# The weights of two wide input products, from the fifth pair on, fetched through ScalarE's DMA queue

## The chip, the cores and the metric

The kernel runs on one core of one Trainium2 chip. The time is the device time of one execution in microseconds; of three runs the median is shown. Lower is better. The core's engines are TensorE (PE, its weight loads PEld), VectorE (DVE), ScalarE (ACT), GpSimd (POOL) and SyncE (SP), which issues all DMAs of this kernel before the change. Each engine takes its instructions strictly in its own order.

## The reference, cut to what matters

Two transformer blocks follow each other on 1024 tokens of width 1024, all in float32: gated linear attention with a pooling branch and a gated feed-forward, then an mLSTM with latent attention and a squared-ReLU MLP. The change touches the first product of each feed-forward part:

```python
gate, up = jnp.split(h2 @ w_ffn_in[l], 2, axis=-1)      # 1024 x 1024 by 1024 x 5632
x = x + (jax.nn.silu(gate) * up) @ w_ffn_out[l]
...
y = jnp.square(jax.nn.relu(m @ w_up[l])) @ w_down[l]    # m @ w_up: 1024 x 1024 by 1024 x 4096
x = x + rmsnorm_2(y, norm_post_mlp[l])
```

## The kernel before, in words

Every float32 factor is split into a high part (rounded to the matmul's format) and the low rest, and a product is three matmuls: high by high, high by low, low by high (`mm3`, lines 117 to 119). The split is a cast on ACT (line 94) and a subtraction on DVE (line 95).

`wide_in` (line 754) does the two wide input products. It is called at line 925 for `w_ffn_in` ("feed-forward" below, 22 pairs of panels) and at line 1687 for `w_up` ("up" below, 16 pairs). A pair is a block of 256 columns of the weight, 1 MB, loaded by one DMA into the tile `raw` (`load`, line 769). The product of the 2 x 2 blocks is done in seven block products of 12 matmuls each, by a scheme that adds and subtracts blocks first. They run in four units: P1 and P2, P5 and P6, P3 and P7, P4 (`UNITS`). Their left operands come from the weight (`operands`): unit 0 from `raw` itself, units 1 and 2 from the sums `s` that POOL makes of blocks of `raw` (lines 808 to 812), unit 3 from `raw`. Each is split into a tile `wo`. The other operands are the blocks of the activations (tiles `b` for P1, P2, P3, tiles `T` for P5, P6, P7, P4), which is how a row of PE shows where P2 ends: the matmul after it reads a `T`.

`product` takes each result out of PSUM, for which there are four banks in turn: P1 and P5 by a copy on ACT into `t` (line 827), P2 by DVE with P1 added (line 832), P6 by DVE (836) with a sum on POOL behind it (838), P3 by DVE with that sum added (841), P7 by DVE (845) and POOL (847), P4 by DVE (851). So DVE's line 841 needs POOL's line 838. Four finished blocks of a pair go through `consume`: in feed-forward a tanh on ACT (line 917) or a product with the gate (line 922), in up a ReLU on ACT and a square on DVE (lines 1683 and 1684). Then `spill_hidden` adds and subtracts them (lines 895 to 905, DVE) and spills seven tiles of 256 KB to DRAM (line 886, `f_scr<-g`) for the product that comes next; in feed-forward every second pair does so.

The program order is that of the loop at line 858: operands run two units ahead of their products, the units 0 of the first four pairs (`PRE`) run first, and the load of the next pair is written ahead of unit 2 (line 865). A scheduler then orders each engine's instructions by a timeline of its own. The tiles `raw` and `wo` come from two pools of three slots of the same size; `W["turn"]` says which. In the steady loop one pool takes, in turn, unit 1 of pair i, `raw` of i + 1, unit 3 of i, unit 0 of i + 1, unit 2 of i + 1, unit 1 of i + 2, `raw` of i + 3. Three slots back from `raw` of i + 3 is unit 0 of i + 1: a load waits until P2 of the pair two before its own has ended.

Of the kernel before, what the change touches and what calls it, by code (L numbers as in the profile page):

```python
# [24 lines left out]
KD = D // P  # L25
# [14 lines left out]
def tile_blocks(ctx, tc, A, out):  # L40
    nc = tc.nc
    act, dve, pool, pe, dma = nc.scalar, nc.vector, nc.gpsimd, nc.tensor, nc.sync
# [37 lines left out]
    def raw_tile(shape, dtype, n):  # L80
        if not W["nraw"]:
            return w_either(shape, dtype, n)
        return W["b"].tile(shape, dtype, tag="raw", name=nm(n), bufs=W["nraw"])
# [26 lines left out]
    def wview(w, k0, kn, c0, cn):  # L110
        return w[k0 * P:(k0 + kn) * P, c0:c0 + cn].rearrange("(k p) n -> p k n", p=P)
# [407 lines left out]
    for h in range(GH):  # L519
# [3 lines left out]
        for _ in range(PANELS[h]):  # L523
            i = next(n_panels)
# [226 lines left out]
    PRE = 4  # L751
    UNITS = (("P1", "P2"), ("P5", "P6"), ("P3", "P7"), ("P4",))

    def wide_in(src, cols, B, consume, side):
# [6 lines left out]
        raws, ts, X = {}, {}, {}  # L761
# [4 lines left out]
        def load(i):  # L766
            W["turn"] = [i % 2]
            raws[i] = raw_tile([P, KD, 256], F32, "raw")
            dma.dma_start(out=raws[i], in_=wview(src, 0, KD, cols[i], 256))

        def combos():

# [85 lines left out]
        for n in range(len(seq) + LEAD):  # L858
            if n == PRE:
                combos()  # L860
            if n < len(seq):
                i, u = seq[n]
                if i not in raws:
                    load(i)
                if u == 2 and i + 1 < len(cols) and i + 1 not in raws:
                    load(i + 1)
                ops[i, u] = operands(i, u)
            if n >= LEAD:
                i, u = seq[n - LEAD]
                w = ops.pop((i, u))  # L870
                for e, p in enumerate(UNITS[u]):
                    product(i, p, w, e)
# [309 lines left out]
    cols = vpl.tile([P, NT, 16], F32, name="cols")  # L1182
# [575 lines left out]
```

## Time and profile before

| | |
|---|---|
| median of three runs | 2745.82 us (2744.04 to 2746.67) |
| profiled execution | 2743.75 us, its span 2742.0 us |
| busy: PE, PEld | 2622.4 us (96%), 2220.5 us (81%) |
| busy: DVE, ACT, POOL | 1770.7, 1138.5, 787.5 us |
| DMA | 314.56 MB, one queue of 35.1% of the engines' time for nearly all of it |
| feed-forward's 22 loads of `raw` | issued from 778.4 to 1217.3 us of the span |
| up's 16 loads of `raw` | issued from 2006.9 to 2376.8 us of the span |

All times in rows count from the start of the span. A row of the timeline gives the start, the duration, the engine, the line, the operation, the tile written and the tiles read, and in brackets how long the engine had been idle and what it waited for. Matmuls overlap: one of 128 x 512 takes 0.39 us and the next starts 0.23 us after it. SPq is the issue of a DMA on SP, not its transfer; the chain of waits has the transfer, as DMA.

### The profile page before, as it was taken

How to read it: one execution, taken by the hardware profiler on the slowest of the kernel's cores; microseconds unless marked ns; L12 is line 12 of the kernel's file. 1: busy time of each engine (PE TensorE's matmuls, PEld its weight loads, DVE VectorE, ACT ScalarE, POOL GpSimd, SP SyncE). 2: the span in 40 equal slices, each digit the busy share in tenths (PEclk: the TensorE clock that was granted, in tenths of full speed). 3: DMA queues.
4: the chain of work that ended last, by engine and by line, in shares of the span. 5: the costliest groups of instructions: out<-in, count | busy, mean ns of one | idle time of the engine just before them, and what ended most of it. 6: DMA issues, size and time to landing. Idle time of an engine off the chain costs nothing.

```text
span 2742.0 us, 36550 instructions
## 1 busy us (share of the span) xinstructions
PE 2622.4 (96%) x13651; PEld 2220.5 (81%) x13651; DVE 1770.7 (65%) x2615; ACT 1138.5 (42%) x2243; POOL 787.5 (29%) x695
## 2 busy tenths in 40 slices
PE   8989999999998999999998999999997998999998
PEld 7879898888896788887887887778895777788887
DVE  4565554474369776766777454388648766676875
ACT  4556665422124332334443432277643332354341
POOL 2333332111106544441013111123336534400014
PEclk9999999999999999999999998899998999999999
DMA  4232222453431333236441332211341433484433
GB/s 136 69 122 62 83 74 92 148 183 124 146 116 54 112 101 111 98 102 235 148 142 68 94 75 79 66 20 42 124 139 62 142 130 128 132 284 152 138 123 131
DMA packets 235889, 314.56 MB, mean 115 GB/s; under 512 B 30048, under 2 KB 157024, under 8 KB 235712
## 3 DMA queue, kind: packets, MB, share of 16 engines
q1 hardware_dynamic: 235712, 312.23, 35.1%
q8 instruction: 108, 1.77, 0.3%
q14 instruction: 69, 0.57, 0.1%
HBM read 220.36 MB, written 91.82 MB: 114 GB/s over the span
## 4 chain that ended last, share of the span: by engine, by line
PE 69%; DVE 12%; DMA 7%; issue 4%; POOL 3%; ACT 3%; SPq 1%; POOLq 0%; DVEq 0%; ACTq 0%
PE psf L119 6%; PE psf L117 6%; PE psf L118 6%; PE pw L1014 5%; PE pw L1015 5%; PE pw L1016 5%; PE pw L117 4%; PE pw L118 4%; PE pw L119 4%; DMA raw<-in_w_up_dram 3%; PE pso L118 2%; PE pso L119 2%; PE pso L117 2%; DMA mb<-m_scr 2%; DVE wo L95 1%
## 5 line engine op out<-in xcount | busy, mean ns | idle before, releaser
L117 PE MATMUL pw<-T,wo 128*128 128x512 f32 x608 | 242.8, 399 | 24.8 <-ACT wo L94 14.4
L1014 PE MATMUL pw<-op 128*128 128x512 f32 x644 | 251.6, 391 | 4.9 <-ACT a L1022 4.9
L1015 PE MATMUL pw<-op 128*128 128x512 f32 x644 | 251.8, 391 | 0.0
L1016 PE MATMUL pw<-op 128*128 128x512 f32 x644 | 251.2, 390 | 0.0
L119 PE MATMUL pw<-T,wo 128*128 128x512 f32 x608 | 238.9, 395 | 4.5 <-DVE wo L95 4.5
L118 PE MATMUL pw<-T,wo 128*128 128x512 f32 x608 | 241.0, 396 | 0.7 <-DVE T L95 0.7
L119 PE MATMUL psf<-hT,w 128*128 128x512 f32 x576 | 227.1, 394 | 0.0
L118 PE MATMUL psf<-hT,w 128*128 128x512 f32 x576 | 226.9, 394 | 0.0
L117 PE MATMUL psf<-hT,w 128*128 128x512 f32 x576 | 226.7, 393 | 0.0
L117 PE MATMUL pw<-b,wo 128*128 128x512 f32 x456 | 181.5, 398 | 18.7 <-DVE c L841 12.9
L119 PE MATMUL pw<-b,wo 128*128 128x512 f32 x456 | 179.5, 395 | 1.0 <-DVE wo L95 1.0
L118 PE MATMUL pw<-b,wo 128*128 128x512 f32 x456 | 179.6, 394 | 0.0
L94 ACT CAST op<-ar 128x1024 fp32r<-128x1024 f32 (+1 forms) x84 | 85.1, 1017 | 193.1 <-PE pw L1016 88.4
L117 PEld LDWEIGHTS pw<-T,wo 128*128 128x128 f32 x608 | 115.8, 190 | 57.8 <-ACT wo L94 15.3
L95 DVE TENSOR_TENSOR op<-ar,op 128x1024 fp32r<-128x1024 f32 (+1 forms) x84 | 100.9, 1204 | 92.4 <-ACT op L94 92.2
L95 DVE TENSOR_TENSOR w<-raw,w 128x1024 fp32r<-128x1024 f32 (+1 forms) x78 | 103.0, 1321 | 84.4 <-ACT w L94 84.1
L1014 PEld LDWEIGHTS pw<-op 128*128 128x128 f32 x644 | 121.6, 189 | 30.8 <-ACT a L1022 5.3
L95 DVE TENSOR_TENSOR wo<-s,wo 128x1024 fp32r<-128x1024 f32 x76 | 126.7, 1668 | 24.5 <-ACT wo L94 24.5
L1015 PEld LDWEIGHTS pw<-op 128*128 128x128 f32 x644 | 121.6, 189 | 25.2
L1016 PEld LDWEIGHTS pw<-op 128*128 128x128 f32 x644 | 121.5, 189 | 25.3
L119 PEld LDWEIGHTS pw<-T,wo 128*128 128x128 f32 x608 | 115.5, 190 | 31.3 <-DVE wo L95 5.9
L118 PEld LDWEIGHTS pw<-T,wo 128*128 128x128 f32 x608 | 115.7, 190 | 26.3 <-DVE T L95 2.0
(481 smaller groups left out, 7304.2 us busy)
## 6 DMA issues: line engine op xcount, KB each, us to landing
f_scr<-g SPq DMA_DIRECT2D x161, 256.0 KB
ar<-f_scr SPq DMA_DIRECT2D x69, 512.0 KB
raw<-in_w_in_dram SPq DMA_DIRECT2D x56, 512.0 KB
raw<-in_w_ffn_in_dram SPq DMA_DIRECT2D x22, 1024.0 KB
raw<-in_w_up_dram SPq DMA_DIRECT2D x16, 1024.0 KB
or<-in_w_down_dram SPq DMA_DIRECT2D x16, 1024.0 KB
or<-in_w_ffn_out_dram SPq DMA_DIRECT2D x10, 1024.0 KB
raw<-in_w_out_dram SPq DMA_DIRECT2D x16, 512.0 KB
```

The source lines that it names most:

```text
L94: act.copy(out=hl_hi, in_=src)
L95: dve.tensor_sub(out=hl_lo, in0=src, in1=hl_hi)
L117: pe.matmul(ps, ah, bh, start=(i == 0), stop=False)
L118: pe.matmul(ps, ah, bl, start=False, stop=False)
L119: pe.matmul(ps, al, bh, start=False, stop=(i == n - 1))
L1014: pe.matmul(ps, ah, bh, start=(si == 0 and k == 0), stop=False)
L1015: pe.matmul(ps, ah, bl, start=False, stop=False)
L1016: pe.matmul(ps, al, bh, start=False, stop=(end and k == q - 1))
```

## The change

In `load`, the DMA of the pairs from the fifth on (`i >= PRE`) is issued by ACT in place of SP: 18 loads of feed-forward, 12 of up. A blank line comes with it, so that the lines behind have numbers higher by one after the change.

```diff
         def load(i):
             W["turn"] = [i % 2]
             raws[i] = raw_tile([P, KD, 256], F32, "raw")
-            dma.dma_start(out=raws[i], in_=wview(src, 0, KD, cols[i], 256))
+
+            (dma if i < PRE else act).dma_start(out=raws[i], in_=wview(src, 0, KD, cols[i], 256))
```

PE, DVE and POOL keep their orders word for word, but for the line numbers. SP keeps the order of all its other DMAs. On SP, in the steady part of up, a load stands among the seven spills of a pair, before:

```order
L886 DMA f_scr<-g_20837 128x512
L886 DMA f_scr<-g_20841 128x512
L886 DMA f_scr<-g_20842 128x512
L769 DMA raw_21032<-in_w_up_dram 128x8x256
L886 DMA f_scr<-g_20817 128x512
L886 DMA f_scr<-g_20870 128x512
```

and after:

```order
L887 DMA f_scr<-g_20837 128x512
L887 DMA f_scr<-g_20841 128x512
L887 DMA f_scr<-g_20842 128x512
L887 DMA f_scr<-g_20817 128x512
L887 DMA f_scr<-g_20870 128x512
```

The load behind `g_20842` is gone, and the spills have closed up. On ACT, in the same part of up (`t` is the copy of P1 or P5, the ReLU `g_20715` is that of P4's block, `g_20760` that of P2's), before:

```order
L94 CAST wo_20852<-s_20849 128x1024
L827 COPY t_20743<-pw_20730 128x512
L1683 ACTIVATE g_20715<-c_20713 128x512
L1683 ACTIVATE g_20760<-c_20758 128x512
L827 COPY t_20780<-pw_20767 128x512
L94 CAST wo_20799<-raw_20722 128x1024
```

and after:

```order
L94 CAST wo_20852<-s_20849 128x1024
L828 COPY t_20743<-pw_20730 128x512
L1684 ACTIVATE g_20715<-c_20713 128x512
L770 DMA raw_20877<-in_w_up_dram 128x8x256
L1684 ACTIVATE g_20760<-c_20758 128x512
L828 COPY t_20780<-pw_20767 128x512
L94 CAST wo_20799<-raw_20722 128x1024
```

The load stands between the ReLU of P4's block and that of the next P2's. On ACT, at the start of feed-forward (the second moved load), before:

```order
L917 ACTIVATE g_8871<-c_8869 128x512
L827 COPY t_8890<-pw_8877 128x512
L94 CAST wo_8986<-s_8983 128x1024
L94 CAST wo_9022<-raw_8848 128x512
L94 CAST wo_9101<-s_9098 128x1024
```

and after:

```order
L918 ACTIVATE g_8871<-c_8869 128x512
L828 COPY t_8890<-pw_8877 128x512
L770 DMA raw_8981<-in_w_ffn_in_dram 128x8x256
L94 CAST wo_8986<-s_8983 128x1024
L94 CAST wo_9022<-raw_8848 128x512
L94 CAST wo_9101<-s_9098 128x1024
```

Here the load comes behind a copy out of PSUM and ahead of a cast.

## Rows read from the trace of the kernel before

**Rows 1.** Windows: stretch, length, busy PE, PEld, DVE, ACT, POOL (count), clock, DMA share

```profile
1009.20:1200.70 191.50, 191.50 (x842) 157.80 (x841) 132.54 (x151) 59.78 (x80) 89.92 (x60) 1.00 0.32 104
2169.90:2369.00 199.10, 179.52 (x758) 141.52 (x757) 129.78 (x153) 61.37 (x91) 82.88 (x57) 0.99 0.40 131
```

**Rows 2.** Timeline, PE: start, us, engine, line, out<-in, [idle before <-releaser]

```profile
2169.83 0.39 PE L117 MATMUL pw<-T,wo 128*128 128x512 f32 x1
...
2368.90 0.39 PE L117 MATMUL pw<-T,wo 128*128 128x512 f32 x1
...
2387.93 0.50 PE L117 MATMUL pw<-b,wo 128*128 128x512 f32 x1 [1.30 <-DVE c L841]
...
2399.99 0.50 PE L117 MATMUL pw<-T,wo 128*128 128x512 f32 x1 [0.88 <-DVE c L832]
```

**Rows 3.** Waits of PE, 2170 to 2404: us in total, times, longest

```profile
PE pw L117 <- DVE c L841: 12.7, 10, 3.6
PE pw L117 <- DVE c L832: 8.4, 10, 1.0
```

**Rows 4.** Chain of waits, one turn of the up product: start, us, what

```profile
2200.24 6.12 DMA raw<-in_w_up_dram
2206.52 1.28 POOL s L808
...
2210.43 0.70 DVE c L841
...
2216.03 0.51 DVE c L851
...
2220.26 0.69 DVE g L895
...
2222.18 6.21 DMA raw<-in_w_up_dram
...
2287.95 8.37 DMA raw<-in_w_up_dram
```

**Rows 5.** Timeline, PE and SP, ahead of one up load

```profile
2192.10 0.39 PE L117 MATMUL pw<-T,wo 128*128 128x512 f32 x1
...
2196.20 3.88 SPq L886 DMA_DIRECT2D f_scr<-g  x3
```

**Rows 6.** Timeline, ACT, behind P4 of an up pair

```profile
2216.85 0.63 ACT L1683 ACTIVATE g<-c 128x512 f32<-128x512 f32 x1
2223.51 0.63 ACT L1683 ACTIVATE g<-c 128x512 f32<-128x512 f32 x1 [6.02 <-DVE c L832]
```

**Rows 7.** Timeline of the feed-forward product: SP, POOL, ACT

```profile
1008.21 0.92 SPq L886 DMA_DIRECT2D f_scr<-g  x2
1009.24 0.41 SPq L769 DMA_DIRECT2D raw<-in_w_ffn_in_dram  x1
...
1025.84 0.38 SPq L769 DMA_DIRECT2D raw<-in_w_ffn_in_dram  x1
...
1015.69 1.29 POOL L808 TENSOR_TENSOR s<-raw 128x512 f32<-128x512 f32 x1 [9.19 <-DMA raw<-in_w_ffn_in_dram]
...
1030.94 1.30 POOL L808 TENSOR_TENSOR s<-raw 128x512 f32<-128x512 f32 x1 [3.86 <-DMA raw<-in_w_ffn_in_dram]
...
1028.52 0.59 ACT L827 COPY t<-pw 128x512 f32<-128x512 f32 x1 [2.83 <-PE pw L119]
```

**Rows 8.** Weight loads on SP by line: shortest, median, longest issue in ns

```profile
L104 SPq DMA_DIRECT2D raw<-in_w_in_dram x80: 367/384/1637, 2.2 to 1726.6; - x80
...
L769 SPq DMA_DIRECT2D raw<-in_w_up_dram x16: 367/384/405, 2006.9 to 2376.8; - x16
```

**Rows 9.** Timeline, start of the feed-forward product: SP, ACT, POOL

```profile
915.46 0.38 SPq L769 DMA_DIRECT2D raw<-in_w_ffn_in_dram  x1
...
918.63 0.57 ACT L827 COPY t<-pw 128x512 f32<-128x512 f32 x1
...
922.42 1.29 POOL L808 TENSOR_TENSOR s<-raw 128x512 f32<-128x512 f32 x1
```

## The prediction

> **What bounds the kernel now.** I read the views in this order: busy time in two stretches of equal work, the waits of PE in the slower one, the chain of waits through it, and then what each engine does around one weight load.
>
> The two wide input products run the same loop: seven block products of 12 matmuls per pair of weight panels. In the first (feed-forward) PE is busy 191.50 of 191.50 us over ten pairs, 842 matmuls; in the second (up) 179.52 of 199.10 us over nine pairs, 758 matmuls, at a granted clock of 1.00 and 0.99 [rows 1]. So a pair costs 19.15 us where PE sets the pace, and 22.12 us in the up product. That stretch has 199.07 us from the first P5 matmul of one pair to that of the ninth after it [rows 2]; at 19.15 it would be 172.35, so 26.7 us are stalls. After the last of these pairs three more stalls come: starts of PE that waited 0.88, 1.30 and 0.88 us (the first and the third are alike, one stands) [rows 2], each followed by about 0.3 us in which the array is refilled (row of 0.50 us in place of 0.39), so some 3.9 us. Together 30.6 us of the up product are not work of PE.
>
> Who ends the stalls: DVE's `c` of line 841 (P3's PSUM) and of line 832 (P2's PSUM), ten times each, 12.7 and 8.4 us [rows 3]; what is missing to the 30.6 is refilling and single waits. DVE is not short of time (129.78 of 199.10 us busy, rows 1); it stands in a ring of waits. The chain shows it [rows 4]: the load of `raw` starts at 2200.24, POOL's line 808 starts at 2206.52, lines 809 and 838 follow in POOL's order, and DVE's line 841, which needs 838, starts at 2210.43. From there DVE and ACT hand each other the next instructions, over line 851 at 2216.03, until line 895 at 2220.26, whose result a spill on SP waits for, and behind that spill the next load starts at 2222.18. One turn is 21.94 us, nearly the pair's 22.12. The loop is bound by where the load stands in SP's queue.
>
> **What moves, and what it is worth.** The change takes the 30 loads of the pairs from the fifth on (18 in feed-forward, 12 in up) from SP to ACT; by the order nothing else on any engine changes place.
>
> *The load in the up product.* Its slot is that of the unit-0 operands two pairs earlier, so it is free when P2 of that pair has ended: the first P5 matmul behind that P2 starts at 2192.10, so about 2192.3 [rows 5]. SP reaches the load only at 2200.24, since from 2196.20 on it stands for 3.88 us in three spills, whose sums DVE makes late in its turn [rows 5]. On ACT the load comes behind the ReLU of P4's `c`: that one starts at 2216.85 and takes 0.63, and then ACT idles 6.02 us until 2223.51 [rows 6]. So the load would start at about 2217.5 in place of 2222.18, 4.7 us earlier in the ring.
>
> *The ring after.* From line 841 to the end of that ReLU: 2217.48 - 2210.43 = 7.05 us. Load to POOL's start: 2206.52 - 2200.24 = 6.28. POOL until line 841: 2210.43 - 2206.52 = 3.91. Sum 17.24 us, under the 19.15 that PE needs. PE then sets the pace. What is late next is the buffer: ahead of PE's P2 the load waits on ACT for its slot. The ring by this path is load 6.28, POOL 3.91, line 841 0.70, P2 about 2.8 us: 13.7, again under 19.15. What is queued behind the waiting load on ACT is the ReLU of P2's own `c`, which needs P2 and DVE's line 832 anyway; so nothing is held by it. The feed-forward product shows that a load that starts when P2 ends is early enough: there POOL waits for its load at 1015.69 and 1030.94 [rows 7] and PE still idles nowhere.
>
> So the 30.6 us go: nine pairs at 19.15, and the three stalls at the end, which are the lag that DVE brought from the ring.
>
> *Unknown: the length of the load on a queue of its own.* No ACT DMA stands in this trace. Bounds from both sides: with no spill right ahead of it, 1025.84 to 1030.94, 5.1 us [rows 7]; with two, 1009.24 to 1015.69, 6.45 us. So a spill costs a load up to 0.65 us; all seven of a pair beside it would give 5.1 + 7 x 0.62, 9.4 us. I take 6.3 to 7, nearest to the rows of the up product itself, for on its new place some three spills (lines 895, 897, 899) fall into it. The ring stays under 19.15 up to a load of 8.2 us. At 9.4 us it is 20.4: nine pairs keep 1.2 each, 11 us, and the three last stalls stay, so some 15 of the 30.6 us remain.
>
> *The issue itself on ACT.* On SP it takes 0.38 us, at most 0.41, in the up loads; the longest of any weight load took 1.64 us [rows 8]. Twelve in the up product fall into the 6 us gap. In feed-forward every second one stands in a gap of 2.83 us ahead of a PSUM copy [rows 7], the others ahead of a tanh that waits for P2 as the load does. At either duration they are covered: 0. If the cover were gone (two ACT instructions back to back), the price is 0.4 to 1.6 us for that load, and PE feels it only where a PSUM bank comes late. Below nothing: SP loses 30 issues, 11.5 us, but no engine waits for SP other than through loads and buffers; 0.
>
> *Feed-forward.* Where PE has no idle time there is nothing to gain. Something can be lost at its start, where ACT comes later to the load than SP did: the second moved load was issued at 915.46 and now stands behind a copy that starts at 918.63 and takes 0.57 us [rows 9], 3.7 us later. It lands at 919.2 + 5.1 = 924.3, and POOL's line 808, at 922.42 before, moves by 1.9 us. That lag is passed on through DVE; the price is between 0 and 1.9 us, since PE has PSUM banks in hand. I take 0.5. Likewise 0.5 for the entry into the up product, whose first loads gain less than the later ones.
>
> Sum against the profiled execution: 2743.75 - 30.6 + 0.5 + 0.5 = 2714.2 us. The median of the runs shown is 2745.82, 2.1 us above it; on that, 2716 us.
>
> **The rivals.**
>
> *The loads come late on the shared engines.* DMA engines are busy a share of 0.40 in the stretch [rows 1], and a load of 8.37 us stands in the chain [rows 4], so longer ones occur. Against it: even all seven spills make 9.4. Time: 2745.8 - 15.6, about 2730 us, the ring turning in 20.4.
>
> *Only the issue is saved.* The load waits for something that comes when SP came to it, and what is gained is SP's own step. For it: nine loads at 0.4 us of issue, 3.4 us, about 2742 us. Against it: the slot is free 8 us before the issue, and ACT idles from 2217.5 on. The Trainium skill speaks for this case (DMA: Bandwidth & Descriptors, Issuing engines are not separate DMA queues): issuing from several engines saves only the sequencer's time to start a transfer, since all run on the same DMA engines. The trace agrees that it isn't bandwidth that is missing (share 0.40), but its SP row stands in waits for DVE and not in issues, and that the rule leaves out.
>
> *ACT is held: slower.* ACT works in order. If an issue there, with its wait, held ACT far longer than on SP, the copy of P5 behind it (1028.52 in rows 7) would come late, and in feed-forward, where PE has nothing to spare, each us is paid in full. The point: that copy frees a bank that PE needs again four products later, three products (8.2 us, at 19.15 / 7 each) after the copy's release, so the hold must exceed 2.83 + 8.2, about 11 us. At 13 us, nine feed-forward pairs pay 2 us each, and the up ring, in which ACT's casts stand, grows by what the gap doesn't cover, 17.24 + 13 - 6.02 = 24.2, 2.1 us over today's for nine pairs: 18 + 19, about 2783 us. Nothing in the trace is near (1.64 at most).
>
> **How the numbers follow.** PE sets the pace in up, 2716: 0.77, by itself 2712 to 2723 (none or 1.9 lost at the start, some small stalls left). Late loads, 2730: 0.12. Only the issue, 2742: 0.06. ACT held, 2783: 0.05. The range takes in the first two and leaves out the rest, 2711 to 2732. A change of under 0.2%, 5.5 us, can't be told from none in these runs. So faster holds the first two, 0.89; same the third, 0.06; slower the fourth, 0.05.
>
> **What the profile after will show.** Right: a second DMA queue, with the 30 loads of 1 MB; PE busy all of a stretch of nine up pairs, which lasts about 172 us; no waits of PE on lines 841 and 832 (their numbers then one higher); POOL's line 808 still waiting for the load, but line 841 within some 5 us of P3's end; feed-forward unchanged at 19.15 us a pair; ACT's issues in what was idle time. Wrong: pairs of 20 to 21 us with loads of over 8 us (the second case), the load at its old distance behind line 895 (the third), or PE waiting for copies of line 827 in feed-forward (the fourth).

## The result, and the profile after

The changed kernel takes 2716.48 us (median; 2714.7 to 2721.35), the kernel before 2746.09 us beside it: a ratio of 0.9892, 95% interval 0.988 to 0.9904. The forecast was 2716. The profiled execution took 2714.7 us, the worked sum 2714.2. All line numbers are one higher than before.

First the two stretches of equal work [rows 1]: length, busy time of PE, PEld, DVE, ACT and POOL with counts, granted clock, DMA share, GB/s.

```profile
1006.60:1198.10 191.50, 191.50 (x842) 157.76 (x841) 133.53 (x150) 60.20 (x80) 94.30 (x60) 1.00 0.30 104
2170.20:2343.60 173.40, 172.83 (x757) 141.70 (x757) 144.85 (x157) 64.95 (x95) 97.80 (x58) 1.00 0.43 152
```

Feed-forward is as it was, busy all of its time. The nine up pairs have shrunk from 199.1 to 173.4 us, and PE's busy time in them is nearly all of it. PE's own timeline for the same pairs [rows 2], between the first P5 matmul of the first and of the tenth pair, with the two waits that lie between:

```profile
2170.25 0.39 PE L117 MATMUL pw<-T,wo 128*128 128x512 f32 x1
...
2176.20 0.50 PE L117 MATMUL pw<-b,wo 128*128 128x512 f32 x1 [0.35 <-ACT t L828]
...
2179.43 0.50 PE L117 MATMUL pw<-T,wo 128*128 128x512 f32 x1 [0.22 <-DVE c L833]
...
2343.69 0.39 PE L117 MATMUL pw<-T,wo 128*128 128x512 f32 x1
```

That is 173.44 us. Both waits lie in the first pair, and they are the only ones up to 2400, where the view of PE's waits had 21.1 us for lines 841 and 832 [rows 3]:

```profile
PE pw L117 <- ACT t L828: 0.3, 1, 0.3
PE pw L117 <- DVE c L833: 0.2, 1, 0.2
```

The chain of waits from 2200 to 2260, by line, where [rows 4] went from the DMA over POOL and DVE back to the DMA; now it is PE and nothing else:

```profile
by line: PE pw L118 33.5%; PE pw L117 33.5%; PE pw L119 33.4%
```

Now one load, on the timelines of ACT, POOL and DVE [rows 4 to 6]:

```profile
2279.01 0.69 DVE L842 TENSOR_TENSOR c<-pw,t 128x512 f32<-128x512 f32 x1 [1.18 <-POOL t L839]
...
2285.45 0.63 ACT L1684 ACTIVATE g<-c 128x512 f32<-128x512 f32 x1
...
2286.45 0.37 ACTq L770 DMA_DIRECT2D raw<-in_w_up_dram  x1
...
2291.66 1.85 POOL L809 TENSOR_TENSOR s<-raw 128x512 f32<-128x512 f32 x1 [2.98 <-DMA raw<-in_w_up_dram]
2291.79 0.64 ACT L1684 ACTIVATE g<-c 128x512 f32<-128x512 f32 x1 [5.71 <-DVE c L833]
...
2295.18 2.30 POOL L839 TENSOR_TENSOR t<-t,t 128x512 f32<-128x512 f32 x1
2297.51 0.69 DVE L842 TENSOR_TENSOR c<-pw,t 128x512 f32<-128x512 f32 x1 [1.19 <-POOL t L839]
```

The pairs are 19.146 us apart, so the P2 that frees the slot ends at 2343.69 - 3 x 19.146 = 2286.25; the load leaves 0.2 us later. It now waits for its slot, no longer for the spills. (So do all loads from 2248.16 on; the three before them left in ACT's turn, 1.6, 0.9 and 0.5 us behind their slot.) POOL starts on the panel 5.21 us later, and the ReLU behind the load waits for P2's result in any case.

The page's queues (packets, MB, share of 16 engines) and the issues of line 770 on ACT (count, shortest, median and longest in ns) [rows 8]:

```profile
q1 hardware_dynamic: 204512, 280.77, 31.1%
q10 hardware_dynamic: 31200, 31.46, 3.7%
```

```profile
L770 ACTq DMA_DIRECT2D raw<-in_w_ffn_in_dram x18: 374/374/431, 897.6 to 1214.7; - x18
L770 ACTq DMA_DIRECT2D raw<-in_w_up_dram x12: 374/374/375, 2140.1 to 2343.9; - x12
```

A second queue carries the 30 loads of 1 MB; an issue costs ACT 0.37 us, where it cost SP 0.38 [rows 8].

**Where the 29 us lie.** PE executes 13,651 matmuls in either trace, in the same order, so the same matmul can be found in both. From the 10,501st (ahead of the up product) to the 12,301st (behind it) before took 420.86 us (2007.76 to 2428.62), after 391.41 (2008.14 to 2399.55): 29.45 less. From the 4,701st to the 6,501st, over feed-forward: 426.57 and 425.89, 0.68 less. All the rest: 1887.25 and 1888.34, 1.1 more; in the 13 traces of this study that rest varies from 1886.7 to 1894.4, though the edits, but for the first loads of act_all, lie outside it. A median is therefore good to some us, but the up stretch can be read to a tenth or two (it is 391.41, 391.42 and 391.42 in three kernels whose up product is the same but for four early loads, 420.86 and 421.02 in two without the change there).

### The profile page after: what moved, and what is told of

Its sections match the earlier page's. It is cut to its first block, busy times and chain, and to the rows that moved or that the text cites. A ratio compares the mean times of both kernels' runs of the same rounds, so it can differ in the third digit from the quotient of the medians.

```text
span 2713.0 us, 36509 instructions
## 1 busy us (share of the span) xinstructions
PE 2611.6 (96%) x13651; PEld 2218.1 (82%) x13651; DVE 1784.4 (66%) x2615; ACT 1140.2 (42%) x2243; POOL 808.7 (30%) x695
## 4 chain that ended last, share of the span: by engine, by line
PE 78%; DVE 10%; DMA 5%; ACT 2%; issue 2%; POOL 2%; SPq 1%; DVEq 0%; POOLq 0%; ACTq 0%
PE pw L117 7%; PE pw L118 7%; PE pw L119 7%; PE psf L117 6%; PE psf L119 6%; PE psf L118 6%; PE pw L1015 5%; PE pw L1016 5%; PE pw L1017 5%; PE pso L118 2%; PE pso L119 2%; PE pso L117 2%; DMA mb<-m_scr 2%; PE py L117 1%; PE py L118 1%
## 5 line engine op out<-in xcount | busy, mean ns | idle before, releaser
L117 PE MATMUL pw<-b,wo 128*128 128x512 f32 x456 | 178.8, 392 | 4.8 <-ACT wo L94 3.1
L119 PE MATMUL pw<-b,wo 128*128 128x512 f32 x456 | 178.1, 392 | 1.8 <-DVE wo L95 1.7
L118 PE MATMUL pw<-b,wo 128*128 128x512 f32 x456 | 178.1, 391 | 0.0
```

Source lines behind the costliest of these rows:

```text
L117: pe.matmul(ps, ah, bh, start=(i == 0), stop=False)
L118: pe.matmul(ps, ah, bl, start=False, stop=False)
L119: pe.matmul(ps, al, bh, start=False, stop=(i == n - 1))
```

## The experiments

Each ratio is to the kernel before as it ran beside that kernel (its medians there were 2744.55 to 2746.67). The table has the up stretch just defined, and the mean of the eight pairs from the 11,384th to the 12,056th matmul (in sp_early1 and act_early1 PE's order inside the stretch is a little different, so their last column is good to a tenth).

| kernel | median us | ratio to before (95%) | up stretch us | one pair us |
|---|---|---|---|---|
| before | 2746.09 | | 420.86 | 22.10 |
| changed | 2716.48 | 0.9892 (0.988-0.9904) | 391.41 | 19.15 |
| up_only | 2716.66 | 0.9892 (0.9877-0.9906) | 391.42 | 19.15 |
| ff_only | 2745.20 | 1.0002 (0.9993-1.0011) | 421.02 | 22.26 |
| sp_early1 | 2712.91 | 0.988 (0.9866-0.9895) | 391.00 | 19.24 |
| act_early1 | 2713.93 | 0.9881 (0.9865-0.9898) | 390.91 | 19.18 |
| both_act | 2734.55 | 0.9961 (0.9945-0.9976) | 409.13 | 20.70 |
| swap_up | 2719.42 | 0.99 (0.9885-0.9915) | 393.01 | 19.15 |
| load_c4 | 2721.31 | 0.9904 (0.9888-0.9921) | 394.81 | 19.15 |
| spill_dup | 2713.85 | 0.9882 (0.9867-0.9896) | 391.13 | 19.15 |
| v_dve | 2715.46 | 0.9884 (0.9869-0.9899) | 391.24 | 19.15 |
| sp_c2 | 2724.45 | 0.9918 (0.9903-0.9933) | 396.89 | 19.34 |
| act_all | 2717.98 | 0.9895 (0.9878-0.9911) | 391.42 | 19.15 |

**One product at a time.**

```diff
-(dma if i < PRE else act).dma_start(
+(dma if i < PRE or len(cols) > 16 else act).dma_start(      # up_only
+(dma if i < PRE or len(cols) == 16 else act).dma_start(     # ff_only
```

> Only the 12 loads of the up product go to ACT, the 18 of feed-forward stay on SP. Theory (the load stood too late in SP's queue in the up product, and nowhere else): all of the gain is here, 2716 us, within 2713 to 2720; nine up pairs in 172.3 us. Rival (the loads gain from a queue of their own wherever they are): part of the gain goes with the 18 loads, some 2728 us by their number (29.6 us x 18/30 kept back).

> Only the 18 loads of feed-forward go to ACT. Theory: PE had no idle time there, so nothing, 2744 to 2748 us, and the up product at 22.1 us a pair as before. Rival (a queue of its own): 2728 us.

All of the gain is the up product's 12 loads; the 18 of feed-forward give no difference in the median. The waits of PE from 2100 to 2420 in ff_only are those of [rows 3]:

```profile
PE pw L117 <- DVE c L842: 13.0, 10, 3.4
PE pw L117 <- DVE c L833: 8.5, 10, 1.0
```

**One queue, but an earlier place; and the same on ACT.**

```diff
-                if u == 2 and i + 1 < len(cols) and i + 1 not in raws:
+                if u == 1 and i + 1 < len(cols) and i + 1 not in raws:
                     load(i + 1)
 # sp_early1: every load by dma (SP); act_early1: as in the changed kernel
```

> One queue: all loads on SP as before, but each is written one unit earlier in the loop, so that it stands ahead of the spills of P4 and of the two sums that DVE makes late, and takes the slot that P4 of the pair before frees; the work of the other engines is reordered a little by it. Theory (the place in the queue counts, not the second queue): PE sets the pace, 19.15 us a pair in up, 2716 us, within 2711 to 2724. Rival (what helped is a second queue beside the spills): no gain, 2740 to 2748 us.

> The loop of the run before, with the loads from the fifth pair on on ACT's queue. Theory: PE is already the bound in both products, so an even earlier load brings nothing more: 2716 us, 2711 to 2722, nine up pairs in 172.3 us. Rival (the load's distance still sets part of the pace): under 2710 us. If the load's wait on ACT held the PSUM copies behind it: over 2725 us, with PE waiting for the copies.

SP in sp_early1, between two loads of the up product:

```profile
2239.01 0.38 SPq L770 DMA_DIRECT2D raw<-in_w_up_dram  x1
2246.86 7.01 SPq L887 DMA_DIRECT2D f_scr<-g  x7
2258.18 0.38 SPq L770 DMA_DIRECT2D raw<-in_w_up_dram  x1
```

All seven spills still stand in one row on SP, 7.01 us, but the load is issued 4.3 us after the last of them (2258.18 - 2253.87), when its slot is free (here that of P4 of the pair before; PE's first matmul behind it starts at 2257.85). With one queue the whole gain is there. What counts is what the load stands behind. act_early1 adds nothing: PE is the bound. sp_early1 has the lowest median of all and act_early1 one of the lowest, but their intervals overlap that of the changed kernel, so they are not shown to be faster than it.

**Which queue, crossed with what else is on it.** In both kernels the up product's spills go to ACT; the loads are on ACT (both_act) or on SP (swap_up).

```diff
-            dma.dma_start(out=scr[OUT_ORDER.index(p), j * P:(j + 1) * P, :], in_=x)
+            (act if n_pairs == 16 else dma).dma_start(out=scr[...], in_=x)
```

> As the changed kernel, but the 98 spills of the up product that go to the hidden layer's scratch stand on ACT's queue too, and two of them, whose sums DVE makes late, ahead of each load. Theory (the place counts): the load is as late as in the kernel before, 22 us or more a pair, 2740 to 2775 us. Rival (a queue other than SP's is what helps the load): 2716 us.

> The same spills on ACT, and the loads back on SP, where nothing that waits for DVE stands ahead of them any more. Theory: the load starts when its slot is free, 19.15 us a pair, 2716 us, within 2712 to 2724; ACT, though held by the spills for DVE's sums, still comes in time with its ReLU (its DVE user stands behind the same sums). Rival (ACT held is paid by PE): PE waits on ACT's casts or copies, over 2730 us.

The load on ACT is late again when the late spills are there too, and on SP it is in time when they are not. This pair is the cleanest of the study: PE, DVE, POOL and ACT execute the same instructions in the same order in both kernels, only the loads' queue differs, and a pair costs 20.70 or 19.15 us. One turn of both_act, on the timelines of DVE, ACT and POOL:

```profile
2262.11 0.69 DVE L898 TENSOR_TENSOR g<-g,g 128x512 f32<-128x512 f32 x1
2262.84 0.33 ACTq L887 DMA_DIRECT2D f_scr<-g  x1
2263.26 0.42 ACTq L770 DMA_DIRECT2D raw<-in_w_up_dram  x1
...
2269.57 1.29 POOL L809 TENSOR_TENSOR s<-raw 128x512 f32<-128x512 f32 x1 [9.18 <-DMA raw<-in_w_up_dram]
2270.82 1.29 POOL L839 TENSOR_TENSOR t<-t,t 128x512 f32<-128x512 f32 x1
2272.07 1.29 POOL L810 TENSOR_TENSOR s<-s,raw 128x512 f32<-128x512 f32 x1
2272.15 0.69 DVE L842 TENSOR_TENSOR c<-pw,t 128x512 f32<-128x512 f32 x1 [3.06 <-POOL t L839]
...
2283.82 0.42 ACTq L770 DMA_DIRECT2D raw<-in_w_up_dram  x1
```

The direction was right, the size (2740 at least) was not: 2734.55. The rows show why. With the spills moved, POOL came out in another order: line 839 now stands between the two sums (809, 839, 810), not behind both. The ring is shorter by one POOL instruction, 21.94 [rows 4] - 1.29 = 20.65 us, and a pair measured 20.70. So the ring fits at a second length.

In swap_up ACT is held by its spills. Its waits between 2170 and 2345:

```profile
ACT g L1684 <- DVE g L896: 18.9, 9, 2.3
```

Nine times some 2 us in front of a ReLU, and yet a pair costs 19.15: a hold of that size on ACT is covered in these pairs. Ahead of them it is not. There ACT stands in spills until 2131.77, its copy and the cast behind it come some 4 us later in the stretch than in the changed kernel, and PE waits for the cast, as in both_act (2.35 us there); of this the stretch keeps 1.6 us:

```profile
2133.26 0.63 PE L117 MATMUL pw<-T,wo 128*128 128x512 f32 x1 [1.81 <-ACT wo L94]
```

**Longer loads, more traffic.**

```diff
+                for q in range(4):                                # load_c4, up only
+                    act.dma_start(out=raws[i][:, :, q * 64:(q + 1) * 64], in_=wview(src, 0, KD, cols[i] + q * 64, 64))
```

```diff
+            if n_pairs == 16:                                      # spill_dup
+                dma.dma_start(out=f2_dup[OUT_ORDER.index(p), j * P:(j + 1) * P, :], in_=x)
```

> As the changed kernel, but each of the 12 loads of the up product is four DMAs of 64 columns, in pieces of 256 bytes, so that the same 1 MB takes longer. Theory from the trace after: with the load's stretch L (issue to the start of POOL's first sum, 5.65 us there), a turn is 6.37 + L + 5.45 us, so PE sets the pace up to L of 7.3 us, and beyond it a pair costs 11.8 + L: at 8.5 us 20.3 and some 2728 us, at 10 us 21.8 and some 2744 us. Rival (by the forecast's own limit of 8.2 us): nothing lost up to there, at 10 us 20.9 a pair and some 2735 us. If the load is out of the ring: 2716 us at any L.

> As the changed kernel, but each of those 98 spills of the up product is written a second time, to a place that nobody reads: 25.7 MB more of traffic beside the loads, on SP's queue. Theory (there is room on the DMA engines): the load's stretch grows by some three spills of 0.62 us, from 5.65 to 7.5 us, just over the limit of 7.3, so 0 to 2 us lost, 2716 to 2720 us. Rival (loads come late on the shared engines): 9.4 us and more, 21.2 us a pair, 2738 us or more.

The nine pairs of spill_dup as a window, to be held against the second row of the changed kernel above:

```profile
2169.10:2342.40 173.30, 172.73 (x758) 141.98 (x757) 139.71 (x156) 65.78 (x94) 90.27 (x58) 1.00 0.69 248
```

DMA share 0.69 in place of 0.43, 248 GB/s in place of 152, and not a tenth of a us lost. There is room on the engines for that much. (POOL has the order 809, 839, 810 here too, so this kernel's ring has 1.3 us more to spare than that of the changed one.)

load_c4 missed its theory. ACT and POOL in it, one turn (774 is the load, 813 the first sum, 843 is the old 838):

```profile
2316.24 1.01 ACTq L774 DMA_DIRECT2D raw<-in_w_up_dram  x2
...
2323.98 1.29 POOL L843 TENSOR_TENSOR t<-t,t 128x512 f32<-128x512 f32 x1 [5.21 <-DVE t L841]
2326.87 1.29 POOL L813 TENSOR_TENSOR s<-raw 128x512 f32<-128x512 f32 x1 [1.60 <-DMA raw<-in_w_up_dram]
```

The first of the four DMAs for the sum at 2326.87 was issued at 2316.24, so the stretch is 10.6 us, and still a pair costs 19.15. The old line 838 now stands in front of the sums, and the load is out of the ring: the third case of the expectation. (The 3.4 us that the stretch is longer lie ahead of the eight pairs: PE waits 0.76 us for line 846 at 2161.57 and 2.03 us for line 837, P2's result, at 2188.52, where the changed kernel waits 0.35 and 0.22 us in all. That it is the longer loads which cost this is not shown.) So the kernel didn't test the limit that it was made for, but it showed another link of the ring, POOL's order, which the next two runs test by itself.

**The same link, with every load on SP.**

```diff
-                pool.tensor_add(out=v, in0=t, in1=ts["P5", i])
+                (dve if len(cols) == 16 else pool).tensor_add(out=v, in0=t, in1=ts["P5", i])   # v_dve; loads by dma
```

```diff
+                for q in range(2):                                # sp_c2, up only; other loads by dma
+                    dma.dma_start(out=raws[i][:, :, q * 128:(q + 1) * 128], in_=wview(src, 0, KD, cols[i] + q * 128, 128))
```

> All loads on SP in their old place; in the up product alone the sum V, on which P3's result waits and which POOL made behind the two sums of the next panel, is made by DVE (16 additions more for DVE, 16 fewer for POOL). Theory (the ring closed over POOL's order: load, two sums of the new panel, V, line 842): it is open now, PE sets the pace or nearly, 19.15 to 19.6 us a pair, 2716 to 2722 us, though each load still stands behind the late spills. Rival (a late load costs PE by itself, through the operands made from it): 22 us a pair, 2740 to 2750 us.

> All loads on SP; the 12 of the up product are two DMAs of 128 columns each, the second of them two spills later than the old place, so the panel is there later than before; with it POOL's order has V ahead of the two sums of the new panel. Theory (POOL's order closes the ring): open, 19.15 us a pair, 2716 us, up to 2722. Rival (the late load itself): 23 us a pair and more, over 2750 us.

SP, DVE and POOL in v_dve:

```profile
2248.36 3.88 SPq L887 DMA_DIRECT2D f_scr<-g  x3
...
2252.35 0.41 SPq L770 DMA_DIRECT2D raw<-in_w_up_dram  x1
...
2255.80 0.69 DVE L839 TENSOR_TENSOR t<-t,t 128x512 f32<-128x512 f32 x1
2257.55 0.69 DVE L842 TENSOR_TENSOR c<-pw,t 128x512 f32<-128x512 f32 x1
...
2258.78 1.29 POOL L809 TENSOR_TENSOR s<-raw 128x512 f32<-128x512 f32 x1 [9.29 <-DMA raw<-in_w_up_dram]
```

SP stands in the three spills for 3.88 us, to the digit as in [rows 5], and the load comes behind them. But line 842 no longer waits for POOL: it is done before the panel has landed, and PE runs at 19.15 us a pair. The load behind the spills cost nothing here; before, it cost because V stood behind it in POOL's order. The load of v_dve is less late, though: it leaves 3.3 us behind its slot (free at 2249.04), against 8.1 before, since DVE, no longer held, makes the spills' sums earlier (SP comes to the three spills 0.7 us ahead of the slot here, and came to them 4.1 us behind it before). sp_c2, where POOL has V ahead of the sums, has it as late as before, with the second half of each panel, which both blocks of POOL's first sum lie in, issued 1.7 us behind the first:

```profile
2205.74 0.47 SPq L774 DMA_DIRECT2D raw<-in_w_up_dram  x1
```

That is 8.2 us behind the slot (2197.51), and a pair costs 19.34. What is left of the late load's price is 0.2 us a pair of the 3. The stretch is 5.5 us longer than that of the changed kernel: 3.2 in the pair ahead of the eight, where PE waits 2.56 us for P2's result at 2184.89 much as in load_c4, 1.5 in the eight, 0.7 behind them. The median, 2724.45, lies 2.5 us over the 2722 expected; in the profiled run the stages that nothing touches took 3.8 us more than in the changed kernel's (1892.2 against 1888.3).

**The first four loads too.**

```diff
-(dma if i < PRE else act).dma_start(
+act.dma_start(
```

> As the changed kernel, but the first four loads of either product go to ACT too. Theory: they are issued long before they are needed and no ring is there yet, so nothing: 2713 to 2720 us, and the up product from its entry to its end as long as in the changed kernel, 391.4 us within 1.5. Rival (the entry waits for these loads behind SP's stores): 3 us or more off.

No difference: the up stretch is the same to 0.01 us. Leaving the first four on SP matters neither way.

## Why the prediction was right

**What bounds the kernel.** Right. 19.15 us a pair where PE sets the pace: measured 19.146 in the up product. The ring is shown by three cuts at three places (the load's queue, the load's place in SP's order, V's place in POOL's order), each of which gives the same 391 us. The text ended with "where the load stands in SP's queue"; that is one link of the ring, and v_dve and sp_c2 show that it costs little or nothing by itself.

**The load in the up product.** Right: free of the spills it waits for its slot, with nothing held behind it. **Its length** was taken as 6.3 to 7 us; from issue to POOL's first sum it was 5.2 to 5.9 where POOL waited for it, near the lower bound.

**The ring after.** Right, and nearly in size, though its parts were not. While the engines make up their lag from the entry, one turn reads:

```profile
2204.21 0.69 DVE L842 TENSOR_TENSOR c<-pw,t 128x512 f32<-128x512 f32 x1 [1.18 <-POOL t L839]
...
2210.58 0.37 ACTq L770 DMA_DIRECT2D raw<-in_w_up_dram  x1
2210.63 0.63 ACT L1684 ACTIVATE g<-c 128x512 f32<-128x512 f32 x1
...
2216.23 1.57 POOL L809 TENSOR_TENSOR s<-raw 128x512 f32<-128x512 f32 x1 [3.20 <-DMA raw<-in_w_up_dram]
...
2220.80 2.14 POOL L839 TENSOR_TENSOR t<-t,t 128x512 f32<-128x512 f32 x1 [1.29 <-DVE t L837]
...
2222.97 0.69 DVE L842 TENSOR_TENSOR c<-pw,t 128x512 f32<-128x512 f32 x1 [1.18 <-POOL t L839]
```

From line 842 to the load it is 6.37 us, not 7.05: the load goes out as the ReLU for P4 starts, not when it has ended. The load's stretch is 5.65, not 6.28. POOL until line 842 is 6.74 less the 1.29 in which it waits for DVE, 5.45, not 3.91 (the last section has why). The sum is 17.47 us, the forecast 17.24: 1.7 us under PE's pace instead of 1.9, by errors that go against each other. What the forecast did not have is that another ring stands nearer to PE. The turn above takes 18.76 us, and the load has no part in it: POOL has its sums 1.29 us before line 839 can start, and what that waits for is DVE, which has worked without a gap from 2208.66 on. That ring is 0.4 us under PE's 19.15. How long a load the load's own ring bears (8.2 us by the forecast, 19.15 - 6.37 - 5.45 = 7.3 by these rows) stays open: both kernels with cut loads came out with another order on POOL.

**Nine pairs, three stalls at the end.** Forecast 30.6 less 0.5 for the entry, 30.1; measured 29.45. The nine pairs took 173.44 in place of 172.35, and the 1.1 us are the first pair's (20.27 us, 2170.25 to 2190.53), where the two short waits above lie. The entry costs 1.1, not 0.5. No stalls follow the last pair, which gives back the 3.9.

**The issue on ACT.** Right: 0.37 us, at most 0.43. PE waits for one copy only, the 0.35 us at 2176.20 shown above; before, the same matmul waited 1.59 us for it.

**The start of feed-forward.** The 0.5 us lost did not come, and no gain is shown either. This trace is 0.68 us shorter than before over the stretch, 0.65 of it at the third moved load. ACT, a row each for the second and third moved load, and POOL's first sum on each [rows 9]; PE runs 1.92 us earlier here than before, from the kernel's first stages:

```profile
916.23 0.37 ACTq L770 DMA_DIRECT2D raw<-in_w_ffn_in_dram  x1
...
930.17 0.38 ACTq L770 DMA_DIRECT2D raw<-in_w_ffn_in_dram  x1
...
921.26 1.28 POOL L809 TENSOR_TENSOR s<-raw 128x512 f32<-128x512 f32 x1 [0.72 <-DMA raw<-in_w_ffn_in_dram]
...
937.38 1.91 POOL L809 TENSOR_TENSOR s<-raw 128x512 f32<-128x512 f32 x1 [7.95 <-DMA raw<-in_w_ffn_in_dram]
```

The second moved load did come later on ACT, by 2.7 us (916.23 + 1.92 - 915.46), and POOL's sum by 0.8, not 1.9; PE lost nothing. The next load, which the forecast did not look at, came earlier, and so did POOL's sum on it, by 2 us. In the kernel before they stood at

```profile
934.89 0.38 SPq L769 DMA_DIRECT2D raw<-in_w_ffn_in_dram  x1
...
941.33 1.29 POOL L808 TENSOR_TENSOR s<-raw 128x512 f32<-128x512 f32 x1 [10.75 <-DMA raw<-in_w_ffn_in_dram]
```

But how long that one load takes varies with the kernel, though its place on ACT does not. From issue to sum it is 7.2 us here, 9.3 in both_act and 9.5 in load_c4 (issued at 933.91):

```profile
943.38 1.29 POOL L813 TENSOR_TENSOR s<-raw 128x512 f32<-128x512 f32 x1 [10.21 <-DMA raw<-in_w_ffn_in_dram]
```

With it the stretch goes from 425.89 us (here and in ff_only) over 426.07 (spill_dup), 426.22 (act_all) and 426.68 (both_act) to 426.93 (load_c4), all with these loads on ACT; with them on SP at their old place it is 426.42 to 426.57 in five kernels. So loads of over 9 us do occur on ACT's queue; why is not shown.

**The sum.** -29.45 - 0.68 + 1.1 = -29.0 on 2743.75 gives 2714.7, against 2714.2. That the two agree to half a us is partly luck: errors of 0.6 and 1.2 us go against each other, the 1.2 is itself within what one load's length moves, and the last 1.1 is the spread of stages that nothing touched.

**The rivals.** Late loads on shared engines: ruled out in the up product, where the moved loads took 5.2 to 5.9 us and 25.7 MB more beside them cost nothing. Only the issue: ruled out by the 29 us, of which 0.4 us a load is the least part. That rule of the Trainium skill (DMA: Bandwidth & Descriptors, Issuing engines are not separate DMA queues) is not contradicted in what it says of bandwidth: sp_early1 has the same gain with one queue. What it leaves out is that a DMA waits on its engine behind whatever waits there. ACT held: did not happen in the changed kernel; in swap_up holds of 2 us cost the pairs nothing and PE 1.8 us once at the entry, and the 11 us from which it should decide were not reached in any run.

## What to carry to other kernels

When a load comes late, look at what it stands behind on its engine's queue before counting bytes: spills that wait for late results hold every DMA after them, and an earlier place in the same queue gave as much here as another queue. Then follow the ring to its end; a late load costs only through an instruction in front of which its consumer stands, here V behind the sums in POOL's order, and the cheapest cut may be there. Compare kernels by the stretch between two matmuls that both execute: here it told a few tenths of a us apart where medians varied by several.

## What the runs showed that I had not expected

- Cutting a load in two or four, writing a spill twice or moving the spills to ACT changed the order that POOL's instructions were given (809, 839, 810 or 839 first), and with it the ring. An experiment that seems to change one thing has to be read with the order of every engine beside it: the expectations of both_act and load_c4 missed for want of it.
- POOL's additions of 128x512 take 1.28 us in [rows 4] and up to 2.30 us after. In the nine pairs before [rows 1], 28 of 56 had no DVE instruction with both inputs in SBUF (the tiles of PSUM are `pw`) beside them and took 1.26 to 1.30 us; the others took 1.29 to 2.27. In the nine pairs after, only 2 of 57 were alone (1.29), and the others took 1.28 to 2.30. DVE pays too. The same line of DVE in the trace after, first where POOL is idle, then beside the sum at 2291.66:

```profile
2224.36 0.69 DVE L1685 TENSOR_TENSOR g<-g 128x512 f32<-128x512 f32 x1 [0.70 <-ACT g L1684]
...
2292.46 1.61 DVE L1685 TENSOR_TENSOR g<-g 128x512 f32<-128x512 f32 x1
```

The Trainium skill (SBUF — State Buffer, SBUF: two separate sides) has the rule: DVE with two SBUF inputs and a POOL instruction that reads SBUF take turns on one pair of ports, and whoever comes second is held for the whole instruction of the other. The trace agrees in these durations; no run here tested it alone. By it the ring's part on POOL grew from 3.91 to 5.45 us when the loads came in time, because DVE's gaps, in which POOL had been alone, were fewer. So a term read from the trace of a stalling loop can be too short for the loop without stalls; here the two other terms, 1.3 us shorter, hid it.
